# Gated linear attention's norm between its scores and states, keys loaded after the scores, and attention scores scaled in three turns

## The chip, the core and the metric

The kernel runs on one core of a Trainium2 chip. TensorE (PE) multiplies matrices, VectorE (DVE), ScalarE (ACT) and GpSimd (POOL) work on tiles, and SyncE (SP) issues nearly all transfers, one after the other in the order of its program. The metric is the device time of one launch in microseconds (us).

## The reference, cut to what matters

One decoder layer: a normed input is projected, differential softmax attention and gated linear attention (GLA) run side by side on the projections, each output is normed and gated, and one matrix projects both back.

```python
h = rms_norm(x, pre_g)
z = jnp.einsum('bsd,de->bse', h, w_in)
qa, ka, va, ga, qb, kb, vb, gb, gk_low = split_columns(z)
# differential attention, 8 heads, two maps each, in blocks of 128 queries
s = jnp.einsum('bqhmd,bkhmd->bhmqk', qb, k).astype(jnp.float32)
p = jax.nn.softmax(jnp.where(mask, s, -jnp.inf), axis=-1)
w = p[:, :, 0] - lam * p[:, :, 1]
out = jnp.einsum('bhqk,bkhv->bqhv', w.astype(v.dtype), v)
# gated linear attention, 4 heads, in chunks
attn = jnp.where(causal, jnp.einsum('bhnik,bhnjk->bhnij', q_dec, k_inv), 0.0)
o_intra = jnp.einsum('bhnij,bhnjv->bhniv', attn, v)
o = jnp.einsum('bhck,bhkv->bhcv', qd, state)
state = state * dl[..., None] + jnp.einsum('bhck,bhcv->bhkv', kt, vc)
ob = rms_norm(ob, gla_g).astype(x.dtype)
ob = ob.reshape(B, S, GLA_WIDTH) * jax.nn.silu(gb)
y = jnp.einsum('bse,ed->bsd', jnp.concatenate([oa, ob], axis=-1), w_out)
return x + rms_norm(y, post_g)
```

The sequence has 1024 rows, the model 1024 columns.

## The kernel before

Sums keep float32 quality by splitting each operand into a rounded part (hi) and a remainder (lo): every product is three matmul passes, hi*hi, lo*hi and hi*lo.

**Projections.** The input projection is a Strassen-like scheme: each pair of column blocks takes seven products of half-size blocks, named x, y and z after the PSUM bank that sums them. A product is twelve matmuls of 128x512. `order` lists the products; `go(n)` runs the next n of them, and after each it advances one background stream by one step. The weights of a product are loaded by SyncE (w_raw), rounded by ScalarE (line 327) and their remainder taken by VectorE (line 329). In the same time the output weights are split and stored back for later (wo_raw, wo_hi, wo_d), and finished projections are stored to DRAM (q_d and k_d for attention, g_d and gg_d for gates, gq_d and gv_d for GLA).

**GLA** is that background stream, the generator `gla()`. It runs over 4 heads with two halves of 512 rows each. Between two of its yields TensorE does one product, so a yield sets how much other work lies between two steps. The steps of a half are: transposed keys (matmuls pk), scores (pa, then masked on GpSimd), two steps of states (kv, added up in gu by VectorE), the norm of the half before (`gla_norm`), two steps of outputs (gpo, copied to the tile go by ScalarE, line 932), and the squares (sq), whose column sums end as a rounded part and remainder in the second half of tile gqd (called hl, line 943). The norm starts with the matmul gms over hl, then ScalarE takes the inverse root, VectorE scales and gates go, and four stores write it, split, to mixe (line 856). When `order` has eight products left, the stream is run to its end without products between.

The GLA tiles have one buffer each: go is in the buffer ks0, the gates gg in ks1, keys and queries kq in q0, decayed queries with hl (gqd) in q1, values gv in k0, masked scores with transposed keys (gan) in k1. The next half's go can be written only when the stores of the present go have read it.

**Attention** follows. It takes over the same buffers for the first head's q, k and ks (the lo/hi swapped keys), so these loads (`load_qk`, lines 964 and 967) wait for GLA's last uses, and SyncE waits with them. Three streams are merged by costs and due times (`merge`): `all_scores` (matmuls sc), `all_values` (transposes wtr, products po) and `out_early` (the output projection of GLA's part, ypart, from the weights wo_hi, wo_lo and the tiles m_hi, m_lo loaded from mixe). For a head's block of 128 queries, `scores` computes both maps; VectorE adds the mask and finds the minimum of the negated scores (line 1124), and ScalarE takes the exponent with its sum (line 1134). `scale_scores` then divides by the sums: a reciprocal, map two scaled on GpSimd by lambda (line 1153), and on VectorE map one scaled less map two (line 1154). A block is scaled in one call, behind the minima of the next block's first map, and its weights w are then free for the values.

TensorE's order is the code's order. On the other engines and SyncE a scheduler orders the instructions by its own simulated times, within their dependences and the places fixed by `issue_after`.

Of the kernel before, what the change touches and what calls it, by code (L numbers as in the profile page):

```python
# [14 lines left out]
P = 128  # L15
# [16 lines left out]
def hymba_kernel(  # L32
# [783 lines left out]
    decay(3)  # L816


    loaded = {}

    def gla_loads(g, half):

        if (g, half) not in loaded:
            qh = kp.tile([P, 2, 512], F32R, tag="q1", name="gqd")
            loaded[g, half] = [None, None, qh]
            if g < GLA_HEADS:
                cs = cols(half)
                kq = kp.tile([P, 2, 512], F32, tag="q0", name="kq")
                v = kp.tile([P, 4, 256], F32, tag="k0", name="gv")
                sp.dma_start(kq[:, 0], gq_d[g][2, :, cs])  # L830
                sp.dma_start(kq[:, 1], gq_d[g][0, :, cs])
                c0 = g % 2 * 256
                sp.dma_start(v, gv_d[g // 2][:, half * 4 : half * 4 + 4, c0 : c0 + 256])
                sp.dma_start(fp(qh[:, 0]), gq_d[g][1, :, cs])
                loaded[g, half][:2] = kq, v
        return loaded[g, half]

    def gla_norm(g, half, o, gates, hl):

# [21 lines left out]
    def gla():  # L861

        norm = None
        gla_loads(0, 0)
        yield
        yield
        for g, half in [(g, half) for g in range(GLA_HEADS) for half in range(2)]:
            cs = cols(half)
            kq, v, qh = gla_loads(g, half)
            qd = fp(qh[:, 0])  # L870
            if half == 0:
                u = None
# [9 lines left out]
            for i in range(4):  # L882
# [36 lines left out]
            for m in range(2):  # L919
# [12 lines left out]
                act.copy(o[:, :, m * 256 : m * 256 + 256], po)  # L932
                free.append(ib)
                yield
            hl = gla_loads(*((g, 1) if half == 0 else (g + 1, 0)))[2][:, 1]
# [159 lines left out]
    def scores(h, qb):  # L1095
# [6 lines left out]
        for m, p in enumerate((p0, p1)):  # L1102
            q = qk[h, "q", qb // 4][:, m, qc]
            parts = parts_of(n)
            if h == DA_HEADS - 1 and (qb, m) in ((1, 1), (0, 0), (0, 1)):

                parts = [(0, 512)]
            for i, (a, b) in enumerate(parts):
                sc = sc_bank("sc", [P, 512])
                for j, name in enumerate(("k", "ks")):  # L1110
                    for half in range(2):
                        lo, hi = max(a, half * 512), min(b, half * 512 + 512)
                        if lo < hi:
                            mm(
                                sc[:, lo - a : hi - a], q,
                                qk[h, name, half][:, m, lo - half * 512 : hi - half * 512],
                                start=(j == 0), stop=(j == 1),
                            )
                e = min(b, n)
                last = i == len(parts) - 1  # L1120

                behind = tc.issue_after(lowest[0]) if (h, qb) == (0, NT - 2) else nullcontext()
                with behind:
                    ins = dve.tensor_tensor_reduce(  # L1124
                        p[:, a:e], sc[:, : e - a],
                        maskt[:, NZ + P - (e - a) :] if last else maskt[:, : e - a],
                        1.0, 3e38 if i == 0 else st[:, 4 + m : 5 + m], ALU.add, ALU.min,
                        st[:, m : m + 1] if last else st[:, 4 + m : 5 + m],
                    )
# [12 lines left out]
                yield c  # L1142

    lowest, unscaled = [], []

    def scale_scores(after):

        if not unscaled:
            return 0.0
        h, qb, n, st, p0, p1 = unscaled.pop()  # L1150
        with tc.issue_after(after.ins) if after else nullcontext():
            dve.reciprocal(st[:, 4:6], st[:, 2:4])  # L1152
            pool.tensor_scalar(p1[:, :n], p1[:, :n], st[:, 5:6], lam, ALU.mult, ALU.mult)  # L1153
            dve.scalar_tensor_tensor(  # L1154
                p0[:, :n], p0[:, :n], st[:, 4:5], p1[:, :n], ALU.mult, ALU.subtract
            )
        w[h, qb] = p0
        return 0.25 + n / 1024 * 1.4

    def all_scores():  # L1160
        for h in range(DA_HEADS):
# [433 lines left out]
```

## Time and profile before

| | us |
|---|---|
| runs: median (lowest to highest, 3 runs) | 1017.77 (1012.45 to 1019.2) |
| the profiled execution, its own time | 1016.52 |
| its span, first to last instruction | 1014.8 |
| VectorE's product of scaled scores (line 1154), 64 of them: busy, and idle before | 53.0, 40.7 |
| ScalarE's copies to go (line 932), 16 of them: busy, and idle before | 8.7, 26.7 |
| TensorE's idle time before gms, two waits | 4.7 |

The profile is of one execution. A row of a stage gives the stretch in us, the sum, and then for TensorE, its weight loads (PEld), VectorE, ScalarE and GpSimd the busy time and in brackets the number of instructions, then the granted TensorE clock (1.00 is full), the share of the transfer engines' time, and GB/s. A row of the timeline gives start, duration, engine, line, operation, output<-inputs and, in square brackets, how long the engine had idled and what released it. SPq rows are SyncE issuing transfers. A row of the waits gives who waited, for whom, and total us, times and longest. In a row of transfers stand count, size and the median us from issue to landing.

### The profile page before, as it was taken

Reading aid. Unit: us, or ns where it says so; the run is one execution under the profiler, and the core shown is the slowest. Engines: PE = TensorE matmul, PEld = TensorE weight load, DVE = VectorE, ACT = ScalarE, POOL = GpSimd, SP = SyncE. Lnnn points to the kernel's source line nnn. Section 1 sums busy time; section 2 is a strip of 40 time slices with the busy share of each in tenths; the row PEclk is TensorE's granted clock in tenths of the full one; section 3 lists DMA queues with packets and bytes.
Section 4 is the critical chain, followed back from the end, with each engine's and each line's share of the span. In section 5 each row is a group of like instructions: output and inputs, shape, how many; then the busy total and the mean of one; then the engine's idle time right before and its main releaser. Section 6 shows DMA issues by size and latency. Waiting matters only on the chain.

```text
span 1014.8 us, 14875 instructions
## 1 busy us (share of the span) xinstructions
PE 967.4 (95%) x4866; PEld 809.3 (80%) x4866; DVE 737.2 (73%) x1450; ACT 589.1 (58%) x1152; POOL 142.0 (14%) x153
## 2 busy tenths in 40 slices
PE   6999999999999999999899889799999999999987
PEld 4878888778888888887788768578888888888765
DVE  5996477888898767867767775477777777777545
ACT  8642232446475476656567764257666667676664
POOL 5410000000000000000000000022222222343242
PEclk9999999999999999999999999899999999999999
DMA  9544333846757776689976779996566589875577
GB/s 334 200 114 150 119 110 110 237 115 161 265 182 242 256 228 220 211 248 289 288 232 213 249 250 317 324 337 204 187 223 214 165 310 352 262 192 96 129 214 139
DMA packets 156845, 220.38 MB, mean 217 GB/s; under 512 B 16240, under 2 KB 83824, under 8 KB 156672
## 3 DMA queue, kind: packets, MB, share of 16 engines
q1 hardware_dynamic: 152736, 212.10, 64.6%
q0 software_dynamic: 4032, 7.34, 4.8%
q8 instruction: 38, 0.62, 0.2%
q14 instruction: 39, 0.32, 0.1%
HBM read 133.93 MB, written 88.60 MB: 219 GB/s over the span
## 4 chain that ended last, share of the span: by engine, by line
PE 67%; DMA 17%; DVE 8%; ACT 4%; issue 3%; SPq 1%; POOL 0%; DVEq 0%; ACTq 0%; POOLq 0%
PE v L117 12%; PE ypart L117 11%; PE x L117 10%; PE z L117 7%; PE y L117 6%; PE sc L117 6%; PE po L117 5%; PE yps L117 4%; PE wtr L120 3%; DMA mixe<-go 2%; DMA v<-v_d 2%; DMA wo_d<-wo_raw 2%; DMA wo_raw<-in_w_out_dram 2%; DMA m_lo<-mixe 2%; DMA ks<-k_d 1%
## 5 line engine op out<-in xcount | busy, mean ns | idle before, releaser
L1134 ACT ACTIVATE p<-p,stt 128x896 f32<-128x896 f32 (+7 forms) x128 | 99.4, 777 | 60.0 <-DVE stt L1124 48.5
L329 DVE TENSOR_TENSOR w<-w_raw,w 128x512 fp32r<-128x512 f32 x134 | 91.4, 686 | 27.2 <-ACT w L327 26.7
L327 ACT CAST w<-w_raw 128x512 fp32r<-128x512 f32 x134 | 82.6, 619 | 39.4 <-PE y L117 19.0
L1153 POOL TENSOR_SCALAR p<-p,stt,lam 128x1024 f32<-128x1024 f32 (+3 forms) x64 | 56.3, 881 | 249.0 <-DVE stt L1152 244.2
L1124 DVE CUSTOM_DVE_ANT_0 p<-sc,maskt 128x512 f32<-128x512 f32 (+3 forms) x128 | 74.5, 586 | 20.5 <-PE sc L117 20.0
L117 PE MATMUL ypart<-wo_hi,m_hi 128*128 128x512 f32 x192 | 80.0, 417 | 5.5 <-issue 5.5
L117 PE MATMUL y<-h_hi,w 128*128 128x512 f32 x320 | 82.0, 399 | 0.6 <-ACT go L932 0.6
L1154 DVE SCALAR_TENSOR_TENSOR p<-p,stt,p 128x1024 f32<-128x1024 f32 (+3 forms) x64 | 53.0, 829 | 40.7 <-POOL p L1153 40.3
L117 PE MATMUL x<-s_hi,w 128*128 128x512 f32 x320 | 80.8, 395 | 1.7 <-ACT s L473 1.6
L117 PE MATMUL z<-s_hi,w 128*128 128x512 f32 x320 | 80.8, 395 | 1.4 <-DVE c L484 1.4
L117 PE MATMUL v<-w,s_hi 128*128 128x512 f32 x256 | 79.3, 390 | 0.6 <-DVE w L285 0.5
L117 PE MATMUL ypart<-wo_hi,m_lo 128*128 128x512 f32 x192 | 76.3, 398 | 0.5 <-DMA m_lo<-mixe 0.5
L117 PE MATMUL ypart<-wo_lo,m_hi 128*128 128x512 f32 x192 | 76.2, 397 | 0.0
L117 PE MATMUL sc<-k,q 128*128 128x512 f32 (+1 forms) x192 | 71.3, 374 | 1.4 <-DVE stt L1124 1.4
L117 PEld LDWEIGHTS x<-s_hi,w 128*128 128x128 f32 x320 | 58.9, 188 | 14.4 <-ACT s L473 2.7
L117 PEld LDWEIGHTS y<-h_hi,w 128*128 128x128 f32 x320 | 60.1, 191 | 12.9 <-ACT go L932 0.8
L117 PEld LDWEIGHTS z<-s_hi,w 128*128 128x128 f32 x320 | 58.9, 188 | 14.0 <-DVE c L484 2.5
L117 PE MATMUL sc<-ks,q 128*128 128x512 f32 (+1 forms) x192 | 66.8, 351 | 2.1 <-DMA ks<-k_d 2.1
L284 ACT CAST w<-w_block 128x1024 fp32r<-128x1024 f32 x24 | 25.2, 1052 | 66.9 <-PE v L117 42.0
L256 DVE TENSOR_TENSOR w_raw<-w_raw 128x512 f32<-128x512 f32 x80 | 55.9, 699 | 11.2 <-DMA w_raw<-in_w_in_dram 10.2
L117 PE MATMUL v<-w,h_hi 128*128 128x512 f32 x192 | 60.3, 401 | 0.7 <-ACT h_hi L567 0.7
L887 POOL TENSOR_SCALAR_AFFINE_SELECT gan<-gan 128x512 f32<-128x512 f32 x8 | 7.1, 888 | 383.7 <-ACT gan L886 383.7
(221 smaller groups left out, 2370.1 us busy)
## 6 DMA issues: line engine op xcount, KB each, us to landing
w_raw<-in_w_in_dram SPq DMA_DIRECT2D x40, 512.0 KB, 4.7
w_block<-in_w_in_dram SPq DMA_DIRECT2D x16, 512.0 KB, 4.1
k_d<-qk_st SPq DMA_DIRECT2D x64, 128.0 KB, 2.4
q_d<-qk_st SPq DMA_DIRECT2D x64, 128.0 KB, 2.7
wo_raw<-in_w_out_dram SPq DMA_DIRECT2D x32, 256.0 KB, 3.1
wo_d<-wo_hi SPq DMA_DIRECT2D x32, 256.0 KB, 2.5
wo_d<-wo_raw SPq DMA_DIRECT2D x32, 256.0 KB, 3.3
q<-q_d SPq DMA_DIRECT2D x32, 256.0 KB, 5.5
```

The costliest lines, as they stand in the source:

```text
L117: tc.keep_in_program_order(pe.matmul(*a, **k))
L120: tc.keep_in_program_order(pe.transpose(dst, src, ident))
L256: dve.tensor_tensor(dst, a, b, ALU.subtract)
L284: act.copy(w[0], src)
L327: act.copy(w[0], src)
L329: split_last[:] = [dve.tensor_tensor(w[1], src, fp(w[0]), ALU.subtract)]
L887: pool.affine_select(a, a, [[0, 4], [1, P]], ALU.is_ge, 0.0, base=0, channel_multiplier=-1)
L1124: ins = dve.tensor_tensor_reduce(p[:, a:e], sc[:, : e - a], maskt[:, NZ + P - (e - a) :] if last else maskt[:, : e - a], 1.0, 3e38 if i == ...
L1134: act.activation(p[:, :n], p[:, :n], AF.Exp, bias=st[:, m : m + 1], scale=-1.0, accum_out=st[:, 2 + m : 3 + m],)
L1153: pool.tensor_scalar(p1[:, :n], p1[:, :n], st[:, 5:6], lam, ALU.mult, ALU.mult)
L1154: dve.scalar_tensor_tensor(p0[:, :n], p0[:, :n], st[:, 4:5], p1[:, :n], ALU.mult, ALU.subtract)
```

## The change

Three edits.

1. In `gla()` the norm of the half before moves from behind the two steps of states to ahead of them, right behind the scores. The place where it stood becomes a bare yield, which every half now has, so each half takes one step more (the first half, which has no norm, too).
2. The keys and queries kq are loaded by a function of their own, `gla_keys`, called for the next half right after a half's scores, where they were loaded with values and decayed queries after the outputs.
3. `scale_scores` keeps a list. A block's reciprocal and GpSimd scaling are issued behind the next block's first map as before, VectorE's product behind the next block's second map, and the weights are released to the values one turn later. The cost that `merge` counts for it now stands with the block's own second map.

```diff
+    def gla_keys(n):
+        g, half = n // 2, n % 2
+        if g < GLA_HEADS and n not in keys:
+            kq = keys[n] = kp.tile([P, 2, 512], F32, tag="q0", name="kq")
+            for i, t in enumerate((2, 0)):
+                sp.dma_start(kq[:, i], gq_d[g][t, :, cols(half)])
...
             pool.affine_select(
                 a, a, [[0, 4], [1, P]], ALU.is_ge, 0.0, base=0, channel_multiplier=-1
             )
+            gla_keys(2 * g + half + 1)
             yield
+            if norm:
+                gla_norm(*norm)
+                yield
             us = [u]
             for m in range(2):
...
                 free.append(ib)
                 yield
-            if norm:
-                gla_norm(*norm)
-                yield
+            yield
             gates = kp.tile([P, 2, 512], F32, tag="ks1", name="gg")
...
                 if last:
-                    c += scale_scores(ins)
+                    scale_scores(ins)
                     if m:
-                        unscaled.append((h, qb, n, st, p0, p1))
+                        scaling.append([0, h, qb, n, st, p0, p1])
+                        c += 0.25 + n / 1024 * 1.4
                 yield c
...
+        done = [x for x in scaling if x[0] == 2]
+        for x in done:
+            scaling.remove(x)
+            w[x[1], x[2]] = x[5]
+        for x in scaling:
+            _, h, qb, n, st, p0, p1 = x
+            with tc.issue_after(after.ins) if after else nullcontext():
+                if x[0] == 0:
+                    dve.reciprocal(st[:, 4:6], st[:, 2:4])
+                    pool.tensor_scalar(
+                        p1[:, :n], p1[:, :n], st[:, 5:6], lam, ALU.mult, ALU.mult
+                    )
+                else:
+                    dve.scalar_tensor_tensor(
+                        p0[:, :n], p0[:, :n], st[:, 4:5], p1[:, :n], ALU.mult, ALU.subtract
+                    )
+            x[0] += 1
...
-        scale_scores(None)
+        for _ in range(3):
+            scale_scores(None)
```

**In the order: TensorE in a half of GLA.** The first rows are before, in the second half of the first head, from the first states to the first output matmul (a product is a row x8 with a row x4 behind it).

```order
L117 MATMUL kv<-gv,gan 128x128 x4
L117 MATMUL y<-h_hi,w 128x512 x8
L117 MATMUL y<-h_lo,w 128x512 x4
L117 MATMUL kv<-gv,gan 128x128 x2
L117 MATMUL z<-s_hi,w 128x512 x8
L117 MATMUL z<-s_lo,w 128x512 x4
L117 MATMUL gms<-gqd,ones 128x512
L117 MATMUL z<-s_hi,w 128x512 x8
L117 MATMUL z<-s_lo,w 128x512 x4
L117 MATMUL gpo<-gan,gv 128x128
```

The same half in the changed kernel, from the norm's matmul on; the next row is the first gpo.

```order
L117 MATMUL gms<-gqd,ones 128x512
L117 MATMUL z<-s_hi,w 128x512 x8
L117 MATMUL z<-s_lo,w 128x512 x4
L117 MATMUL kv<-gv,gan 128x128 x4
L117 MATMUL z<-s_hi,w 128x512 x8
L117 MATMUL z<-s_lo,w 128x512 x4
L117 MATMUL kv<-gv,gan 128x128 x2
L117 MATMUL x<-s_hi,w 128x512 x8
L117 MATMUL x<-s_lo,w 128x512 x4
L117 MATMUL y<-h_hi,w 128x512 x8
L117 MATMUL y<-h_lo,w 128x512 x4
```

Between gms and the first gpo stood one product, and now stand four products and both kv groups.

**TensorE and SyncE at GLA's end.** Before, the last gpo of all was followed by these rows up to the last gms; fourteen products came after it.

```order
L117 MATMUL gpo<-gqd,gu 128x128
L117 MATMUL x<-s_hi,w 128x512 x8
L117 MATMUL x<-s_lo,w 128x512 x4
L117 MATMUL y<-h_hi,w 128x512 x8
L117 MATMUL y<-h_lo,w 128x512 x4
L117 MATMUL x<-s_hi,w 128x512 x8
L117 MATMUL x<-s_lo,w 128x512 x4
L117 MATMUL x<-h_hi,w 128x512 x8
L117 MATMUL x<-h_lo,w 128x512 x4
L117 MATMUL gms<-gqd,ones 128x512
```

The same in the changed kernel; eight products come after it.

```order
L117 MATMUL gpo<-gqd,gu 128x128
L117 MATMUL y<-h_hi,w 128x512 x8
L117 MATMUL y<-h_lo,w 128x512 x4
L117 MATMUL z<-s_hi,w 128x512 x8
L117 MATMUL z<-s_lo,w 128x512 x4
L117 MATMUL gms<-gqd,ones 128x512
```

Four products stood between the last gpo and the last gms, and now two. SyncE before, from GLA's last two stores on; ten loads of wo follow (the last row is the first), then m_hi, m_lo and the eight stores of k_d.

```order
L856 DMA mixe<-go 128x4x128 x2
L967 DMA ks_5607<-k_d 64x512 x2
L393 DMA g_d<-g_st 128x512
L967 DMA ks_5607<-k_d 64x512 x2
L654 DMA wo_raw<-in_w_out_dram 128x512
L383 DMA q_d<-qk_st 64x512 x4
L967 DMA ks_5612<-k_d 64x512 x3
L650 DMA wo_d<-wo_hi 128x512
L967 DMA ks_5612<-k_d 64x512
L650 DMA wo_d<-wo_raw 128x512
L997 DMA wo_hi<-wo_d 128x1024
```

SyncE in the changed kernel at the same place (the first rows are the last of twelve loads of wo).

```order
L1004 DMA wo_hi<-wo_d 128x1024
L1004 DMA wo_lo<-wo_d 128x1024
L860 DMA mixe<-gg 128x4x128 x2
L860 DMA mixe<-go 128x4x128 x2
L1021 DMA m_hi<-mixe 128x1024
L1021 DMA m_lo<-mixe 128x1024
L383 DMA k_d<-qk_st 64x512 x8
L974 DMA ks_5607<-k_d 64x512 x4
L974 DMA ks_5612<-k_d 64x512 x4
```

The wo loads moved ahead of the last stores, the ks loads behind m and the k_d stores.

**VectorE at the start of attention.** Before, from the minima of the second block's first map on (p_5864 and p_5865 are the first block's maps; ISA rows with p are minima, those with stt alone read them out).

```order
L1124 ISA p_5891,stt<-sc,maskt,stt 128x384
L1124 ISA stt 128x1
L1152 RECIPROCAL stt<-stt 128x2
L1154 SCALAR_TENSOR_TENSOR p_5864<-p_5864,stt,p_5865 128x1024
L1124 ISA p_5892,stt<-sc,maskt 128x512
```

And in the changed kernel.

```order
L1131 ISA p_5897,stt<-sc,maskt,stt 128x384
L1131 ISA stt 128x1
L1164 RECIPROCAL stt<-stt 128x2
L1131 ISA p_5898,stt<-sc,maskt 128x512
L1131 ISA stt 128x1
L1131 ISA p_5898,stt<-sc,maskt,stt 128x384
L1131 ISA stt 128x1
L1169 SCALAR_TENSOR_TENSOR p_5864<-p_5864,stt,p_5865 128x1024
```

The second map's two minima now stand between the reciprocal and the product.

More of the change, by code (lines that the diff above doesn't have):

```diff
@@ L816, in hymba_kernel, with gla_loads @@
     decay(3)
[L819 to L825, printed above, removed]
+    keys, loaded = {}, {}
+    def gla_keys(n):
[4 more added lines that the diff above has]
+                sp.dma_start(kq[:, i], gq_d[g][t, :, cols(half)])
+    def gla_loads(n):
+        g, half = n // 2, n % 2
+        if n not in loaded:
+            v, qh = None, kp.tile([P, 2, 512], F32R, tag="q1", name="gqd")
             if g < GLA_HEADS:
-                cs = cols(half)
-                kq = kp.tile([P, 2, 512], F32, tag="q0", name="kq")
                 v = kp.tile([P, 4, 256], F32, tag="k0", name="gv")
-                sp.dma_start(kq[:, 0], gq_d[g][2, :, cs])
-                sp.dma_start(kq[:, 1], gq_d[g][0, :, cs])
                 c0 = g % 2 * 256
                 sp.dma_start(v, gv_d[g // 2][:, half * 4 : half * 4 + 4, c0 : c0 + 256])
-                sp.dma_start(fp(qh[:, 0]), gq_d[g][1, :, cs])
-                loaded[g, half][:2] = kq, v
-        return loaded[g, half]
+                sp.dma_start(fp(qh[:, 0]), gq_d[g][1, :, cols(half)])
+            loaded[n] = v, qh
+        return loaded[n]
     def gla_norm(g, half, o, gates, hl):
@@ L868, in gla @@
             cs = cols(half)
-            kq, v, qh = gla_loads(g, half)
+            (v, qh), kq = gla_loads(2 * g + half), keys[2 * g + half]
             qd = fp(qh[:, 0])
@@ L1138, in scores @@
                 if last:
-                    c += scale_scores(ins)
+                    scale_scores(ins)
                     if m:
-                        unscaled.append((h, qb, n, st, p0, p1))
+                        scaling.append([0, h, qb, n, st, p0, p1])
+                        c += 0.25 + n / 1024 * 1.4
                 yield c
-    lowest, unscaled = [], []
+    lowest, scaling = [], []
     def scale_scores(after):
[L1148 to L1158, printed above, removed]
+        done = [x for x in scaling if x[0] == 2]
[15 more added lines that the diff above has]
+            x[0] += 1
     def all_scores():
```

5 lines of the change are left out of this document (3 added, 2 removed).

## The prediction

> **What bounds the kernel now.** I read the page's busy shares first, then the busy time by stage, the list of what TensorE waited for, and then the timeline around each of those waits.
>
> ```profile
> PE 967.4 (95%) x4866; PEld 809.3 (80%) x4866; DVE 737.2 (73%) x1450; ACT 589.1 (58%) x1152; POOL 142.0 (14%) x153
> 500.00:550.00 50.00, 46.55 (x253) 39.63 (x252) 36.19 (x60) 33.15 (x62) 2.12 (x2) 1.00 0.73 241
> 550.00:600.00 50.00, 41.97 (x206) 34.64 (x206) 37.85 (x63) 36.49 (x68) 0.89 (x1) 0.98 0.76 246
> 600.00:650.00 50.00, 44.06 (x180) 35.50 (x180) 25.87 (x42) 18.21 (x31) 0.00 (x0) 0.92 0.92 313
> 690.00:850.00 160.00, 159.99 (x937) 139.15 (x936) 120.19 (x328) 108.75 (x241) 39.16 (x41) 1.00 0.67 225
> ```
>
> TensorE is the bound: 967.4 of 1014.8 us (the second column of a stage row is its busy time, the column before the last two the granted clock). The change adds and removes no matmul, so all that can be won is TensorE's idle time, 47 us in all, and clock lost after it. None of it lies in the middle of attention (159.99 of 160 us busy). 11.5 lie in the second half of GLA (500 to 600) and 5.9 where GLA ends and attention begins; the rest lies mostly before GLA and in the last 70 us, which the change doesn't touch. What ended the waits:
>
> ```profile
> PE gms L117 <- DVE gqd L943: 4.7, 2, 4.1
> PE kv L117 <- ACT go L932: 3.3, 1, 3.3
> PE kv L117 <- DMA gv<-gv_d: 2.7, 1, 2.7
>   DMA mixe<-go: 24.8, 6
> 540.77 0.40 PE L117 MATMUL gms<-gqd,ones 128*128 128x512 f32 x1
> 558.32 1.08 SPq L856 DMA_DIRECT2D mixe<-go  x1
> 564.71 1.07 ACT L932 COPY go<-gpo 128x512 f32<-128x512 f32 x2 [6.41 <-DMA mixe<-go]
> 565.35 1.16 PE L117 MATMUL kv<-gv,gan 128*128 128x128 f32 x8 [3.30 <-ACT go L932]
> 573.04 0.47 PE L117 MATMUL gms<-gqd,ones 128*128 128x512 f32 x1 [0.59 <-DVE gqd L943]
> 584.42 0.44 SPq L856 DMA_DIRECT2D mixe<-go  x1
> 589.51 1.08 ACT L932 COPY go<-gpo 128x512 f32<-128x512 f32 x2 [3.07 <-DMA mixe<-go]
> 596.85 0.69 DVE L943 TENSOR_TENSOR gqd<-sq,gqd 64x512 fp32r<-64x512 f32 x1
> 597.59 0.63 PE L117 MATMUL gms<-gqd,ones 128*128 128x512 f32 x1 [4.13 <-DVE gqd L943]
> 598.01 3.48 PE L117 MATMUL y<-h_hi,w 128*128 128x512 f32 x8
> 607.87 2.72 PE x L117 x12
> ```
>
> The fourth row is from the view of tile go: ScalarE's copies of the outputs into go stood still 24.8 us, six times, until the stores of the previous half's normed outputs had read the one go buffer. What ScalarE has queued behind such a copy (mask inputs, sums, weights) is late too. TensorE's idle from there: 3.3 before kv at 565.35; 2.7 before another kv, whose mask copy stood in ScalarE's queue behind such a go copy (the row blames gv's transfer); 0.59 at 573.04; 4.13 before the last gms; and 0.5 and 0.6 in two smaller cases. That is 11.8 us. After the 4.13 us the next eight matmuls took 3.48 instead of 2.07 us, 1.4 us of clock: 13.2 us together.
>
> **The change, part by part.** *The norm moves up.* Its number of instructions and transfers stays (per half one gms, two reads, four stores). From gms to the copy that its stores let go, 573.04 to 589.51, are 16.5 us. Today TensorE does one product between gms and the next gpo, 2.7 us by the last row above, and has the copy's input ready some 5 us after gms. Changed, four products (10.9), two kv groups and the gpo group lie between, about 14 us. So the wait shrinks from 11 us to some 2, which other work behind gpo covers; I leave 1.5 us in for halves whose stores are slow. gms itself now follows the last gpo by four products in all halves but the last, 10.9 us; the chain from go copy to gqd took 8.0 (589.51 to 597.54). That holds.
>
> *The last gms.* Each half has one step more, so the interleaving runs out later: after the last gpo there are now two products (5.4 us) before the last gms, where there were four. Without the wait in front, the chain of 8.0 us starts at once, half a microsecond shorter since only one copy is left: 7.5 - 5.4 = 2.1 us of stall. ScalarE's queue decides the rest: nothing if it is emptier than at 589.51, up to 7 if the cast of wo_hi that stands inside the chain waits for its load. I take 2.5. Whether the clock drops after it is open; after 1.87 us of idling it did:
>
> ```profile
> 948.85 0.51 PE L117 MATMUL yps<-wo_hi,m_hi 128*128 128x512 f32 x1 [1.87 <-ACT yps L1447]
> 951.58 0.63 PE L117 MATMUL yps<-wo_lo,m_hi 128*128 128x512 f32 x1
> 952.84 0.40 PE L117 MATMUL yps<-wo_lo,m_hi 128*128 128x512 f32 x1
> ```
>
> At 951.58 a matmul takes 0.63 us, at 952.84 0.40 again. I count 1.4 us, as after the 4.13. The Trainium skill, "TensorE: Matmul & The Clock Gate", section "What's actually happening", has the clock halve only after an idle window of about 3.4 us; by it this 1.4 would be 0 and the forecast 1001.6; the row at 948.85 speaks against it here, and the row decides. GLA so: 13.2 - 1.5 - 2.5 - 1.4 = 7.8 us gained, between 3 (stall of 7) and 13.2 (nothing left).
>
> *Keys.* The same two transfers per half, issued once pa has read the old ones rather than with the values. No wait of TensorE on kq is in the trace, so the gain is nothing; they leave the moment of gv, gqd and the stores, and SyncE runs in order: bounds 0.5 us to either side.
>
> *Where GLA ends.* The last norm now stands eight products before the first ypart instead of fourteen, and SyncE's order turns round: weights wo first, then the last stores of mixe, mixe's loads m at once, the eight k_d stores, and only then the eight ks loads.
>
> ```profile
> 611.06 1.36 SPq L856 DMA_DIRECT2D mixe<-go  x2
> 612.52 1.42 SPq L967 DMA_DIRECT2D ks<-k_d  x2
> 633.35 0.32 SPq L1014 DMA_DIRECT2D m_hi<-mixe  x1
> 628.95 1.35 DVE L379 SCALAR_TENSOR_TENSOR qk_st<-c,qk_st 128x512 fp32r<-128x512 f32 x2
> 635.80 9.11 SPq L383 DMA_DIRECT2D k_d<-qk_st  x8
> 643.27 0.77 PE L117 MATMUL ypart<-wo_hi,m_hi 128*128 128x512 f32 x1 [5.48 <-issue]
> 644.49 0.79 PE L117 MATMUL ypart<-wo_hi,m_lo 128*128 128x512 f32 x1 [0.46 <-DMA m_lo<-mixe]
> 645.00:650.00 5.00, 5.00 (x15) 3.87 (x14) 0.70 (x2) 0.00 (x0) 0.00 (x0) 0.60 0.87 258
> 650.00:655.00 5.00, 5.00 (x23) 3.92 (x22) 3.44 (x11) 3.20 (x5) 0.56 (x1) 1.00 0.96 353
> 630.85 0.32 SPq L997 DMA_DIRECT2D wo_hi<-wo_d  x1
> ks<-k_d SPq DMA_DIRECT2D x64, 128.0 KB, 6.0
> ```
>
> Today the products end at 637.8 (643.27 less the 5.48) and attention starts at 643.27: 5.9 us idle (5.48 that the profile calls issue, but in which m was still landing, and 0.46), then 15 matmuls in 5 us where 23 is the rate, 1.7 us, and 0.8 on the first two: 8.4 us. The loads of m left only at 633.35, behind ks loads that waited for go and gates to be stored and behind ten wo loads. Changed: stores about 9 to 12 us after the last gms (573.04 to 584.42 is 11.4), m issued behind them and landed by 18 to 20, products done at 22.2 (0.4 and eight times 2.72). So m should be there. The ks loads are late next: their stores' data come from the fourth product after gms, 11.3 us, and today are done 3.4 us after it (630.3, four products before 637.8), so 14.7. Eight stores at 0.5 us end at 18.7; of the ks loads the first score wants the fifth and sixth, out at 21 and in at 27 with the 6.0 us of the last row. TensorE, six ypart and one sc matmul after its products, asks at 23.8. 3.3 us idle, 3.5 with a little clock: gain 4.9 us. Bounds: 8.4 (ks in time) and a loss, for which see the rivals.
>
> *Scores scaled in three turns.* The same 64 reciprocals, 64 POOL scalings and 64 VectorE products; the product no longer stands right behind POOL's scaling but behind the second map's minima.
>
> ```profile
> DVE p L1154 <- POOL p L1153: 40.3, 41, 1.4
> 655.68 1.29 DVE L1154 SCALAR_TENSOR_TENSOR p<-p,stt,p 128x1024 f32<-128x1024 f32 x1 [1.35 <-POOL p L1153]
> 657.63 0.38 PE L117 MATMUL sc<-k,q 128*128 128x256 f32 x1 [1.39 <-DVE stt L1124]
> 663.97 0.63 PE L120 MATMUL wtr<-ident,p 128*128 128x128 f32 x4 [1.71 <-DVE p L1154]
> 680.57 0.47 PE L117 MATMUL sc<-ks,q 128*128 128x512 f32 x1 [0.59 <-DMA ks<-k_d]
> 610.00:690.00 80.00, 70.36 (x339) 57.83 (x338) 44.55 (x110) 33.97 (x70) 8.34 (x9) 0.96 0.96 325
> ```
>
> VectorE's 40.3 us of waiting for POOL go, and nearly all of it is worth nothing, since TensorE has no gap there. Only the two gaps at the start hang on it: 1.39 us before sc (minima behind the first wait for POOL), and 1.71 before wtr, where the product is behind one minimum more but without POOL in front. I take 1.5 off the two; at most 3.1 off, at worst 1 more for a later product. wtr keeps its places in TensorE's order, score products move back by about ten, so the values find their weights as before; if that cover failed, each of the 32 groups of values could cost up to the 1.3 us of a product, but wtr waits once in the whole trace, so I count nothing.
>
> The sum: 7.8 + 4.9 + 1.5 = 14.2 us off the profiled execution's 1016.5 gives 1002.3. That execution is 1.3 us below the median of 1017.77, so 1003 us against the median.
>
> **The rivals.** *The copies still wait.* From the gms at 540.77 to its last store at 558.32 went 17.5 us, more than the 14 now between; and DMA shares of 0.73 to 0.92 in these stages won't fall if the same bytes pass in less time. Then GLA gains its lower bound 3, the join 4.9: 1016.5 - 7.9, and 1.3 for the median, about 1010. For it: copies wait six times today. Against it: the room before gpo grows by three products in every half.
>
> *The transfers are the bound.* From 610 to 690 the DMA engines are 0.96 busy, and at 680.57 TensorE waits for the second head's ks. If that landing doesn't move, all gained before it is given back there: 1016 to 1018. Against it: in the new order the twelve wo loads stand before the last stores, not behind them, so part of these 26 MB (80 us at 325 GB/s) moves ahead, where shares of 0.73 and 0.76 leave room.
>
> *Slower: the last norm is too late.* Today last gms to first ypart takes 45.7 us (597.59 to 643.27). With eight products behind it only 22.2 us are covered. If that chain stayed 45.7, TensorE would idle 23.5 us, with 2.5 of clock 26, where 8.4 are lost now: 17.6 lost against 9.3 gained, 1026. It decides from a chain of 37 us on. For it: the k_d stores, behind which ks now stands, took 9.11 us for eight. Against it: between stores and m stood 20 us of other issues, which are gone from there, and that pace came from the backlog of wo loads at 630.85.
>
> **How the numbers follow.** The forecast, 1003, with its own bounds from 993 (13.2, 8.4 and 3.1 gained) to 1009 (3, 4.9 and 0.5): 0.62. Copies still wait, 1010: 0.18. Transfers bind, 1017: 0.12. Last norm too late, 1026: 0.08. About 1%, 10 us, can be told from no change here: faster means below 1007.6, slower above 1028. Of the forecast 0.55 lies below 1007.6, of the second case 0.07: faster 0.62. Slower is only the far part of the last case, 0.05, and the same 0.33. The range 994 to 1017 leaves out the last case, half of the third, and a little below.
>
> **What would show it.** Right: the waits of go copies on mixe below 8 us in place of 24.8; no idle over 2 us in GLA but for the last gms; first ypart within 2 us of the last product, ks the next wait; VectorE's wait for POOL near zero, with no change of TensorE's busy time between 690 and 850. Wrong: a last gms that stalls over 5 us; a first score that waits over 8 us for ks; the second head's ks landing as late as now.

## The result, and the profile after

The changed kernel took 1008.08 us (median of 8 runs, 1004.3 to 1015.33); the kernel before, in the same series, 1018.49 us (8 runs, 1012.45 to 1022.74). The ratio is 0.9899, 95% interval 0.9864 to 0.9934. In a second series it was 0.9951 (0.9924 to 0.9977): 1009.39 us (12 runs) against 1015.55 (33 runs). The changed kernel came to 1008 to 1009 both times; it is the kernel before that lay between 1014.5 and 1018.5 from series to series. So the change is worth 6 to 10 us, and the forecast's 1003 was 5 to 6 us too low. The profiled execution took 1006.61 us, its span 1004.9, against 1016.52 and 1014.8 before.

Busy time after, first over the span and then by stage (columns as before the change):

```profile
PE 964.7 (96%) x4866; PEld 809.7 (81%) x4866; DVE 737.9 (73%) x1450; ACT 589.9 (59%) x1152; POOL 144.0 (14%) x153
```

```profile
500.00:550.00 50.00, 48.83 (x253) 41.21 (x252) 38.39 (x61) 37.04 (x70) 1.61 (x2) 1.00 0.75 245
550.00:600.00 50.00, 49.66 (x266) 42.37 (x264) 40.68 (x68) 34.99 (x65) 0.63 (x1) 1.00 0.80 259
600.00:650.00 50.00, 40.06 (x161) 31.93 (x161) 26.33 (x55) 19.42 (x33) 2.28 (x2) 0.93 0.96 324
690.00:850.00 160.00, 158.68 (x927) 138.49 (x926) 118.44 (x328) 110.11 (x242) 44.89 (x45) 1.00 0.72 237
```

The second half of GLA, 500 to 600, idles 1.5 us where it idled 11.5. The next 50 us idle 9.9 where they idled 5.9. The border flatters the first pair: the wait before the last gms lies ahead of 600 in the kernel before (4.13 us, ended at 597.59) and behind it now. From 500 to 650 together it is 11.4 us in place of 17.4. What ended TensorE's waits, VectorE's and ScalarE's (who waited, for whom: us, times, longest):

```profile
PE gms L117 <- DVE gqd L950: 6.2, 2, 5.1
PE sc L117 <- DMA ks<-k_d: 6.1, 2, 4.0
PE wtr L120 <- DVE p L1169: 2.9, 2, 1.7
DVE p L1169 <- POOL p L1165: 12.2, 16, 2.4
  DMA mixe<-go: 11.6, 5
```

Two waits of TensorE are new in size, the one before the last gms and the one for ks; VectorE's wait for GpSimd fell from 40.3 to 12.2 us, and the go copies' wait from 24.8 to 11.6. TensorE's timeline at those places, and ScalarE's between the last go copy and the last gms:

```profile
604.74 0.79 PE L117 MATMUL gms<-gqd,ones 128*128 128x512 f32 x1 [5.07 <-DVE gqd L950]
605.33 3.33 PE L117 MATMUL x<-s_hi,w 128*128 128x512 f32 x8
609.41 2.00 PE L117 MATMUL x<-s_hi,w 128*128 128x512 f32 x8
...
628.48 0.39 PE L117 MATMUL ypart<-wo_hi,m_hi 128*128 128x512 f32 x1
634.66 0.47 PE L117 MATMUL sc<-ks,q 128*128 128x512 f32 x1 [4.04 <-DMA ks<-k_d]
635.79 0.63 PE L117 MATMUL ypart<-wo_hi,m_hi 128*128 128x512 f32 x1
```

```profile
594.79 0.60 ACT L939 COPY go<-gpo 128x512 f32<-128x512 f32 x1
596.98 0.62 ACT L327 CAST w<-w_raw 128x512 fp32r<-128x512 f32 x1 [1.59 <-PE y L117]
601.34 0.62 ACT L646 CAST wo_hi<-wo_raw 128x512 fp32r<-128x512 f32 x1 [2.16 <-DMA wo_raw<-in_w_out_dram]
601.98 0.62 ACT L947 COPY sq<-sq 64x512 f32<-64x512 f32 x1
603.35 0.62 ACT L949 CAST gqd<-sq 64x512 fp32r<-64x512 f32 x1
```

The last gms comes 9.95 us after its go copy began; inside that stand a cast of w, which waited 1.59 us for TensorE's product y, and a cast of wo_hi, which waited 2.16 us for a transfer; neither has anything to do with GLA. After the 5.07 us the next eight matmuls take 3.33 us instead of 2.00. The products end at 628.48, where they ended at 637.8, and m is there at once; ks is not. SyncE at that place:

```profile
618.58 3.72 SPq L1021 DMA_DIRECT2D m_hi<-mixe  x1
622.87 5.23 SPq L383 DMA_DIRECT2D k_d<-qk_st  x8
```

The ks loads follow at 628.15.

### The profile page after: what moved, and what is told of

Its sections match the earlier page's. It is cut to its first block, busy times and chain, and to the rows that moved or that the text cites. A ratio compares the mean times of both kernels' runs of the same rounds, so it can differ in the third digit from the quotient of the medians.

```text
span 1004.9 us, 14892 instructions
## 1 busy us (share of the span) xinstructions
PE 964.7 (96%) x4866; PEld 809.7 (81%) x4866; DVE 737.9 (73%) x1450; ACT 589.9 (59%) x1152; POOL 144.0 (14%) x153
## 4 chain that ended last, share of the span: by engine, by line
PE 73%; DMA 9%; DVE 8%; ACT 4%; issue 3%; SPq 1%; POOL 1%; DVEq 0%; ACTq 0%; POOLq 0%
PE x L117 13%; PE v L117 12%; PE ypart L117 11%; PE y L117 8%; PE z L117 8%; PE sc L117 6%; PE po L117 5%; PE yps L117 4%; PE wtr L120 2%; PE gpo L117 2%; DMA w_raw<-in_w_in_dram 2%; DMA k<-k_d 1%; PE kv L117 1%; DMA v_d<-v_hi 1%; DMA wo_d<-wo_raw 1%
## 5 line engine op out<-in xcount | busy, mean ns | idle before, releaser
L1165 POOL TENSOR_SCALAR p<-p,stt,lam 128x1024 f32<-128x1024 f32 (+3 forms) x64 | 61.4, 960 | 204.7 <-DVE stt L1164 190.4
L117 PEld LDWEIGHTS y<-h_hi,w 128*128 128x128 f32 x320 | 59.0, 188 | 11.6
L256 DVE TENSOR_TENSOR w_raw<-w_raw 128x512 f32<-128x512 f32 x80 | 55.7, 698 | 11.8 <-DMA w_raw<-in_w_in_dram 10.7
L473 ACT COPY s<-x 128x512 f32<-128x512 f32 x60 | 34.9, 581 | 48.4 <-PE x L117 44.0
L1169 DVE SCALAR_TENSOR_TENSOR p<-p,stt,p 128x1024 f32<-128x1024 f32 (+3 forms) x64 | 53.5, 836 | 12.5 <-POOL p L1165 12.2
```

Of the source, the lines that this page charges most:

```text
L117: tc.keep_in_program_order(pe.matmul(*a, **k))
L256: dve.tensor_tensor(dst, a, b, ALU.subtract)
L473: act.copy(b[k], ps)
L1169: dve.scalar_tensor_tensor(p0[:, :n], p0[:, :n], st[:, 4:5], p1[:, :n], ALU.mult, ALU.subtract)
```

## The experiments

The table has three series on three chips, each with the kernel before on the same chip. "Products end" is the moment in the profiled execution when the last product before attention is done (the first ypart's start less its idle time), and "then" what remains of the span.

| kernel | median us | before | ratio (95%) | products end | then |
|---|---|---|---|---|---|
| norm alone | 1010.82 | 1014.53 | 0.997 (0.995 to 0.999) | 632.6 | 371.4 |
| keys alone | 1021.04 | 1014.53 | 1.0074 (1.0048 to 1.01) | 639.3 | 385.0 |
| scores' turns alone | 1014.07 | 1014.53 | 1.000 (0.9978 to 1.0021) | 636.9 | 375.1 |
| norm and keys | 1011.06 | 1014.53 | 0.9973 (0.9951 to 0.9995) | 633.5 | 376.7 |
| the whole change again | 1009.39 | 1015.55 | 0.9951 (0.9924 to 0.9977) | 633.8 | 374.9 |
| norm and scores' turns | 1011.95 | 1015.55 | 0.9961 (0.9935 to 0.9986) | 633.3 | 371.2 |
| whole, ks ahead of k_d | 1009.09 | 1015.55 | 0.9941 (0.9914 to 0.9968) | 635.4 | 374.7 |
| whole, no empty step | 1007.91 | 1015.55 | 0.9927 (0.9902 to 0.9953) | 623.6 | 381.0 |
| that, ks behind m | 1006.35 | 1016.60 | 0.9905 (0.9876 to 0.9934) | 625.1 | 378.3 |
| that, last wo behind ks too | 1006.94 | 1016.60 | 0.9904 (0.9879 to 0.9929) | 627.1 | 380.9 |
| norm alone, no empty step | 1008.71 | 1016.60 | 0.9922 (0.9898 to 0.9945) | 626.1 | 380.6 |

The first execution of the whole change ended its products at 628.5 and needed 376.4 us then; the kernel before 637.8 and 377.0. One profiled execution is uncertain by some us: the same GLA code ended its products at 628.5 and at 633.8, 5.3 us apart. And the profiled executions of the norm alone and of norm and scores' turns were the fastest of their series, 5 to 6 us under the median, those of the keys alone and of the last wo behind ks the slowest, 5 and 3 us over it.

**The parts by themselves.** The norm with its extra step, the keys and the scores' turns were each put into the kernel before; a fourth kernel is the whole change without the scores' turns. The edit of the first:

```diff
@@ before: gla()
+            if norm:
+                gla_norm(*norm)
+                yield
             us = [u]
...
-            if norm:
-                gla_norm(*norm)
-                yield
+            yield
```

> Only the norm's move (with the step it adds to each half); keys and scores as before. Theory A (norm carries all, the scores' turns cost a little): 9 to 12 us below the kernel before, so at or 1 to 2 us under the whole change; the waits of go copies on mixe near 11.6 us as in the whole change. Theory B (the forecast's split: scores worth 1.5 us, norm the rest): 8 to 9 us below before, 1 to 2 us over the whole change. Theory C (the keys must come sooner or the moved norm can't pay): under 5 us below before, with a wait of TensorE's on kq in GLA that neither kernel has.

> Only the keys' transfers are issued sooner. Theories A and B: within 1 us of before, go copies still waiting about 25 us on mixe. Theory C gives no gain here either, but then the move of the norm alone must fall short. A loss of 2 us or more would say that the sooner keys delay gv or the stores.

> Only the scaling of the scores in three turns. Theory B: 1.5 us below before, from the gaps of 1.39 and 1.71 us at the start of attention. Theory A: 0 to 2 us above before, since the second turn's product stands later than the weights' transposes want it (waits of wtr on p summing to over 2.5 us instead of 1.71). Both: VectorE's 40.3 us of waiting for POOL falls to some 12, and TensorE's busy time from 690 to 850 stays within 1 us of 160.

> The norm's move and the sooner keys, scores scaled as before. Theory A: 10 to 12 us below before, 0 to 2 us under the whole change. Theory B: 8 to 9 us below before, 1 to 2 us over the whole change. If it equals the norm's move alone within 1 us, the keys are worth nothing here.

The norm alone gives 1 to 5 us, less than theory A or B expected. Theory C named that size, but its mark, a wait on kq, isn't in the trace, and adding the keys (0.9973) changes nothing. The keys alone cost 5 to 10 us. In GLA the trace shows one cause, a wait for values that left later (before, the longest such wait was 2.7 us). SyncE, and then TensorE:

```profile
463.25 5.70 SPq L383 DMA_DIRECT2D k_d<-qk_st  x8
470.17 0.40 SPq L837 DMA_DIRECT2D gv<-gv_d  x1
475.10 2.04 PE L117 MATMUL kv<-gv,gan 128*128 128x128 f32 x8 [5.99 <-DMA gv<-gv_d]
```

The values stood behind eight stores of k_d; in the kernel before, the same half's had left at 460.88, ahead of those stores. So the sooner keys changed the order of SyncE's queue, and they are not themselves what the values waited for. That and the other waits put the products' end 1.5 us later; the other 8 us of this execution, 5 us over its median, lie in attention, and why the sooner keys would bring those stayed open.

The scores' turns alone are worth nothing, between 2.2 us less and 2.1 more. TensorE's waits there:

```profile
PE wtr L120 <- DVE p L1162: 2.9, 2, 1.7
PE po L117 <- DVE wt_lo L1201: 1.7, 4, 0.6
PE wtr L120 <- DVE wt_lo L1201: 0.9, 1, 0.9
PE sc L117 <- DVE stt L1124: 0.5, 1, 0.5
```

The gap before sc shrank from 1.39 to 0.49 us, as was hoped. But wtr keeps its 1.71 and waits a second time, 1.2 us, and the transposes' copies (wt_lo), behind the later products on VectorE, are waited for by 2.6 us. Some 0.9 us won against 3.8 of new small waits; the runs can't tell the remainder from nothing.

**The whole change again, and without the keys.** Parts of 0.997, 1.007 and 1.000 don't make 0.9899, so the whole change was run again, and the norm with the scores' turns:

> The whole change once more, unaltered, in one series with the other three here, since norm and keys without the scores' turns came to a ratio of 0.9973 on one chip while the whole change had 0.9899 in its own series, and the scores' turns alone had 1.000. Theory A (three parts that add up: norm 3 to 4 us, keys nothing, scores nothing, and the rest of the 10 us was the series): 0.995 to 0.999, that is 2 to 5 us below before. Theory D (the parts help each other: the scores' turns are worth 7 us only once the norm has moved): 0.988 to 0.992, that is 8 to 12 us below.

> The norm's move and the scores in three turns, keys loaded where they were. Theory A: the norm's move alone, 2 to 5 us below before. Theory D: as the whole change, 8 to 12 us below, if the keys are worth nothing; 2 to 5 below only if the keys are what the scores' turns need, for which no mechanism is known.

The whole change came to 0.9951 and the pair to 0.9961, as theory A had it. There is no interplay of 7 us; most of the difference was the level of the kernel before in the first series. The repeat's GLA (TensorE's timeline, with its ks wait):

```profile
516.91 0.47 PE L117 MATMUL gms<-gqd,ones 128*128 128x512 f32 x1 [2.67 <-DVE gqd L950]
609.04 0.80 PE L117 MATMUL gms<-gqd,ones 128*128 128x512 f32 x1 [5.46 <-DVE gqd L950]
633.82 0.39 PE L117 MATMUL ypart<-wo_hi,m_hi 128*128 128x512 f32 x1
638.75 0.76 PE L117 MATMUL sc<-ks,q 128*128 128x512 f32 x1 [2.79 <-DMA ks<-k_d]
```

and the two go copies that these gms hang on (ScalarE):

```profile
505.11 0.59 ACT L939 COPY go<-gpo 128x512 f32<-128x512 f32 x1
598.88 0.60 ACT L939 COPY go<-gpo 128x512 f32<-128x512 f32 x1
```

From copy to gms are 11.8 and 10.2 us, not 8.0.

**The ks loads ahead of the stores they don't need.** The whole change, with the first head's ks loads issued behind m and their place fixed:

```diff
@@ whole change: before attention
-    for n in ("q", "k", "ks"):
+    for n in ("q", "k"):
...
     mix0 = mix(0)
+    for half in (1, 0):
+        load_qk(0, "ks", half)
     go(3)
```

> The whole change, with the first head's eight ks loads issued right behind the loads of m and ahead of the eight k_d stores, which they don't need. If the ks wait of 4.04 us in the join comes from standing behind those stores (5.23 us on the queue): the wait falls under 1.5 us, its slow matmuls go with it, and the time falls 3 to 6 us against the whole change. If the ks loads are held by the last mixe stores or by the DMA engines being full: the wait stays within 1 us and the time within 1.5 us.

The ks wait is gone, and with it the slow matmuls. The time hardly moved (1009.09 against 1009.39): what was won is waited out 21 us later, for the first values.

```profile
637.37 0.39 PE L117 MATMUL sc<-ks,q 128*128 128x512 f32 x1
...
658.88 0.55 PE L117 MATMUL po<-wt_hi,v 128*128 128x256 f32 x1 [3.56 <-DMA v<-v_d]
```

So the cause of the ks wait was the k_d stores, as expected, but removing it was worth nothing, which neither side had foreseen.

**Without the empty step.** The bare yield where the norm stood is left out, so four products stand again between the last go copy and the last gms, and fourteen behind it.

```diff
@@ whole change: gla()
                 free.append(ib)
                 yield
-            yield
             gates = kp.tile([P, 2, 512], F32, tag="ks1", name="gg")
```

> The whole change without the empty step that each half got, so that again four products stand between the last go copy and the last gms, and fourteen behind it. Theory A for the end of GLA: the stall at the last gms and the ks wait are one thing, a chain from the last go copy to ks with too few products beside it; with four more beside it the 5.07 us and its 1.3 us of clock go, the ks wait falls under 1 us, and the time falls 6 to 11 us against the whole change, unless the go copies wait longer on mixe again (over 16 us in all). Rival: what is won at gms comes back at the first ypart, which waits 3 to 6 us for m as in the kernel before: 2 to 5 us below the whole change.

> Only the norm's move, without the empty step, keys and scores as before: the smallest edit that might hold the whole gain. If the empty step costs what the last gms loses and the keys give nothing: as the whole change without that step, 0.991 to 0.994. If the keys' earlier loads are what lets half after half start in time once the empty step is gone: 0.996 to 1.000, with waits of kv on gv or of pk on kq in GLA over 2 us in all.

The stall at the last gms vanishes, and the products end 10 us sooner than in the repeat, at 623.6. Not only do four products cover the chain from go copy to gqd again, it is also shorter, 6.0 us (575.60 to 581.59). Then TensorE stands before m, whose loads left at 619.84 behind four ks loads and five of wo, and the rival came about, if with a smaller gain:

```profile
628.02 0.47 PE L117 MATMUL ypart<-wo_hi,m_hi 128*128 128x512 f32 x1 [4.47 <-DMA m_hi<-mixe]
```

For m_lo it waits another 1.24 us. In time this kernel can't be told from the whole change (1007.91 and 1009.39, the intervals overlap). The norm alone without the empty step has 0.9922 (to 0.9945) against 0.997 (from 0.995) with it. These intervals miss each other by 0.0005, and they come from two series on two chips, while the whole change differed by 0.005 between two series; so that the empty step costs time is likely and not shown. In that smallest edit the go copies wait on mixe as much as before the change, and TensorE's GLA still runs 11.7 us faster:

```profile
  DMA mixe<-go: 24.8, 7
```

**m, ks and wo in the order in which they are wanted.** To the kernel without the empty step came the ks edit above; in a second kernel also the last four wo loads of twelve went behind ks.

```diff
@@ second kernel
-    for e in range(E, E + 6):
+    for e in range(E, E + 4):
         weights(e)
...
+    weights(E + 4)
+    weights(E + 5)
     go(3)
```

> The whole change without the empty step, and the eight ks loads issued behind the loads of m. Without the ks loads in front of them the loads of m leave 3 us earlier than in the run without the empty step (there m_hi left at 619.84 and landed at 628.02). Theory E (the join is set by SyncE's order alone): the first ypart's waits of 4.47 and 1.24 us shrink to under 3 together, with under 1 us on ks, and the time falls 2 to 5 us below the kernel without the empty step, to a ratio of 0.987 to 0.991. Theory F (behind the join the queue of SyncE and the memory tiles of v are the bound, so that time won at the join is waited out before the first values): the join's waits shrink as said, but po then waits 3 to 6 us for v and the ratio stays at 0.991 to 0.994.

> As the run with m before ks, and the last four of the twelve wo loads (2 MB) behind ks too, so that m leaves right after its stores. Theory E: no wait over 1 us at the first ypart, 0 to 3 us for ks, ratio 0.983 to 0.988. Theory F: no wait at the first ypart either, but waits for v of 4 to 8 us, and a ratio of 0.990 to 0.994, the same as without the empty step.

Theory F came about, if with slightly lower ratios. The waits at the join fall from 5.7 us to 1.9 and 0.8 in the first kernel and to 1.4 for ks in the second, and the first values wait longer instead. The first kernel, TensorE, and then SyncE:

```profile
627.43 0.50 PE L117 MATMUL ypart<-wo_hi,m_lo 128*128 128x512 f32 x1 [1.93 <-DMA m_lo<-mixe]
627.77 0.40 PE L117 MATMUL ypart<-wo_lo,m_hi 128*128 128x512 f32 x1
629.88 0.47 PE L117 MATMUL sc<-ks,q 128*128 128x512 f32 x1 [0.80 <-DMA ks<-k_d]
653.07 0.55 PE L117 MATMUL po<-wt_hi,v 128*128 128x256 f32 x1 [5.15 <-DMA v<-v_d]
```

```profile
628.88 5.23 SPq L383 DMA_DIRECT2D k_d<-qk_st  x8
...
636.27 7.31 SPq L383 DMA_DIRECT2D q_d<-qk_st  x8
643.68 2.48 SPq L383 DMA_DIRECT2D k_d<-qk_st  x4
646.25 2.48 SPq L383 DMA_DIRECT2D q_d<-qk_st  x4
648.78 1.07 SPq L1084 DMA_DIRECT2D v<-v_d  x2
```

In the second kernel the same po waits 6.79 us. In all four kernels without the empty step v leaves between 648.8 and 649.8, whether the products ended at 623.6 or at 627.1. In the first execution of the whole change, products done at 628.48, it left at 648.97 as well, and there no po waited for it. Behind k_d SyncE issues without a pause for 20 us, and the transfer engines are full meanwhile (the first kernel by stretches, the share before the last column):

```profile
630.00:643.00 13.00, 12.51 (x57) 10.05 (x57) 9.01 (x28) 6.28 (x11) 2.29 (x2) 1.00 0.91 283
643.00:649.00 6.00, 3.21 (x19) 2.59 (x18) 4.22 (x12) 2.81 (x7) 0.99 (x1) 1.00 0.93 269
649.00:653.00 4.00, 0.00 (x0) 0.00 (x0) 1.02 (x2) 0.51 (x2) 0.00 (x0) 0.73 0.96 297
```

**Fewer, larger stores.** Is it the number of issues or the bytes that hold v back? In the first of those kernels the last q and k stores were written as one transfer for both halves of the partitions:

```diff
@@ m and ks first: take()
-                for m in range(2):
-                    ins = sp.dma_start(d[m, t, :, cs], fp(src)[64 * m : 64 * m + 64])
+                if ending:
+                    tc.keep_in_program_order(sp.dma_start(d[:, t, :, cs], fp(src)))
```

> The run with m and ks first, with the queue's last stores of q and k, 24 of 128 KB each behind m, written as 12 of 256 KB (both halves of the partitions in one). In that run v left at 648.78, behind 20 us in which the queue issued k_d, wo, q_d, k_d and q_d stores without a pause, and po waited 5.15 us for it. Theory F1 (the queue issues too many transfers, 0.65 us each): v leaves 5 to 9 us earlier, po's wait falls under 1.5 us, and the ratio falls by 0.003 to 0.006, to 0.985 to 0.988. Theory F2 (the same bytes take their time on the DMA engines, or v waits for the stores to land): each merged store takes twice as long on the queue or v stays put, po still waits 4 us or more, ratio 0.989 to 0.992.

Neither theory: 1053.42 us, ratio 1.0366 (1.0328 to 1.0404). TensorE stood 40.9 us before the first values, and a merged store took five times as long on the queue as a half, not twice.

```profile
647.19 17.92 SPq L383 DMA_DIRECT2D q_d<-qk_st  x4
665.21 8.47 SPq L383 DMA_DIRECT2D k_d<-qk_st  x2
673.77 12.15 SPq L383 DMA_DIRECT2D q_d<-qk_st  x2
```

```profile
665.00:686.00 21.00, 0.00 (x0) 0.00 (x0) 0.00 (x0) 0.00 (x0) 0.00 (x0) 0.50 0.13 51
```

From 665 to 686 SyncE issues nothing but these stores, and 0.13 of the sixteen engines' time is busy, as much as two engines have. The target of such a store is a block of 2 by 64 by 512. The Trainium skill, "DMA: Bandwidth & Descriptors", section "Rules for kernel authors", says that an outermost dimension smaller than 16 confines a transfer to at most as many engines as it has entries, here 2 of 16, or 0.125; the row agrees. The kernel thus measures another thing than it was meant to, and whether issues or bytes hold v back stays open; the full engines of 630 to 653 speak for the bytes.

## Why the prediction was right, and where it was off

The direction and the range held (994 to 1017); the size did not. Of the 14.2 us that were added up, 6 to 10 came, which is at the bound of 1% in the one series and under it in the other. (The sum gives 1003.6; it was rounded down to 1003.) That the first series came nearest is in part luck: the kernel before was 3 us slower there than in the second.

The miss shows when the sum is split by place. Up to the products' end 7.8 us were forecast, and behind it 6.4, 4.9 for the join and 1.5 for the scores. In the first execution 9.3 and 0.6 came (377.0 behind it became 376.4), in the repeat 4.0 and 2.1. In both the part behind the products' end fell short, and in the repeat GLA's part too.

**The norm moves up: the gain is there, one price was too low.** In the five other executions with the norm moved and the empty step the products' end moved by 2.4 to 5.2 us, in the first by 9.3. The step that failed in GLA is "the chain from go copy to gqd took 8.0 (589.51 to 597.54). That holds": one instance, from a place where no cast that isn't part of the chain made it wait in ScalarE's queue. It measured 9.95 and 10.2 us at the last gms, 11.8 in a middle half of the repeat, and 6.0 without the empty step. So the last gms stalled 5.07 and 5.46 us and not 2.5 (within the 7 that was named for a cast of wo_hi that waits, which is part of what the first trace shows). A stall over 5 us was a named sign of being wrong, and it came in all six executions (5.07 to 5.74). A middle half, which was to be covered, stalled another 2.67: its last copy began 3.2 us after the last gpo, since the other copy of the pair had waited 2.09 us for mixe, and the chain took 11.8, against 12.3 us of TensorE's work beside both. The clock term was right: 3.33 us less 2.00 is 1.3, against 1.4.

One reading of the kernel before was wrong: the 2.7 us before kv were put down to a mask copy behind a go copy. In the code kv reads the transposed keys and the values, not the masked scores. The keys' copy had ended at 500.92; gv had left at 498.05, and its loads take 5.7 us in the median. So the row that blames gv was right, and these 2.7 us were not the go copies'.

**The empty step was costed as a stall, and was worth more at the products' end.** Without it the products end 10.7 to 14.2 us sooner than before, near the whole 13.2 that was called removable. The prediction did see that the step takes two products from the front of the last gms; the traces show that this, with the longer chain, is what separates the kernels with it from 13.2. In the time of the whole kernel no such difference is shown.

**The marker was wrong.** The forecast wanted the go copies' waits below 8 us. They were 11.6, and in the kernel with the norm alone and no empty step 24.8 as before, with the products done 11.7 us sooner. So "the wait shrinks from 11 us to some 2" is not the step on which the gain hangs. The reading that fits, though no run tests it, is that the move buys not a copy that waits less, but more matmuls that TensorE has to do between gms and the work behind the copy. For the same reason the rival "the copies still wait", whose 1010 is nearer to the 1008 to 1009 measured than 1003, has the number by luck: where the copies waited as long as before, GLA was not slower for it.

**The join** was forecast at 3.5 us left of 8.4. Left were 4.04 us and about 1.5 of clock in the first execution (the matmuls of 0.63 us from 635.79 to 638.78 come every 0.43 us instead of every 0.23), so that 2.9 us were gained and not 4.9, and 2.79 in the repeat, with slow matmuls behind it too. The step that failed is "Eight stores at 0.5 us end at 18.7": they ended 23.4 us after the last gms, since they left at 622.87, behind m's loads, the first of which held the queue for 3.72 us, and took 0.65 each. The order of causes was as told, m there, ks late behind the k_d stores, which the kernel with ks in front of them shows.

**The scores' three turns** were forecast at 1.5 us off and are worth nothing that can be measured. "wtr waits once in the whole trace, so I count nothing" failed: the cover of the values was thin just there, and the later product is waited for at wtr and, through VectorE's queue, at wt_lo. Between 690 and 850, where TensorE had idled nothing, it now idles 1.3 us.

**The keys** cost nothing with the norm moved, as forecast; alone they cost 5 to 10 us.

**The rival "the transfers are the bound"** had 0.12, and part of it came. It was looked for at the second head's ks. There it bit in the first execution, 2.07 us where it had been 0.59, with a clock of 0.94 from 660 to 690 in place of 1.00:

```profile
668.86 0.47 PE L117 MATMUL sc<-k,q 128*128 128x512 f32 x1 [2.07 <-DMA ks<-k_d]
```

With the eight slow matmuls behind it, up to 673.02, that costs some 3 us by estimate, about what the join had won. Yet this ks came 11.7 us sooner than before, so it did not land "as late as now", and in the repeat it held up nothing there. In the kernels without the empty step the transfers bite sooner: at m (5.7 us in the whole change without it), and, where m comes in time, at the first values (5.15 and 6.79). The column "then" of the table agrees: kernels whose products end at 623 to 627 need 378 to 381 us then, the ones that end at 632 to 635 need 371 to 377. These differences are not much larger than what one execution is uncertain by.

**The clock.** The slow matmuls after the last gms came after an idle time of 5.07 us. In the kernel with norm and scores' turns they came after 2.63 (granted clock 0.84 from 635 to 640):

```profile
635.09 0.40 PE L117 MATMUL sc<-k,q 128*128 128x512 f32 x1
638.11 0.48 PE L117 MATMUL sc<-ks,q 128*128 128x512 f32 x1 [2.63 <-DMA ks<-k_d]
638.82 0.63 PE L117 MATMUL ypart<-wo_hi,m_lo 128*128 128x512 f32 x1
```

After the 1.93 us at 627.43 above, the next ypart took 0.40, and in the kernel before, after the 3.30 us at 565.35, the next eight matmuls of 128x512 took 2.09 us together, the full rate. So the length of the one idle time does not decide it here. The Trainium skill, "TensorE: Matmul & The Clock Gate", section "What's actually happening", has the clock halve only after an idle window of about 3.4 us; the 2.63 us here don't bear that out, as the 1.87 in the prediction did not.

No version is shown to beat the whole change: the best two, 1006.35 and 1006.94 us, have ratios of 0.9905 and 0.9904, whose intervals overlap both of its own.

## What to carry to other kernels

Before a gain upstream is counted, look for the first point downstream whose time is set by something else (here ks, m or the first values, behind a full queue of transfers), and count only up to it. Price a chain through a shared engine from several of its instances, not from one, since what the scheduler puts between its links belongs to its length. And when a step of an interleaving is moved, look at the number of steps: an empty one changes what stands beside the last, uncovered chain (here 10 us at the products' end, of which nothing that can be told was left in the time of the whole kernel).

## What the runs showed that was not expected

Two stores of 64 by 512 written as one of 2 by 64 by 512 made the queue take 4.5 us for each (17.92 for four) where each half had taken 0.9 (7.31 for eight), at 51 GB/s from 665 to 686 against some 270 to 280 in the kernel with the halves, and the kernel came out 38 us over the kernel before. And the kernel before, unaltered, had medians of 1018.49, 1014.53, 1015.55, 1016.60 and 1015.03 us in five series, the last four on four chips: a ratio of 0.99 from one series of 8 runs was 0.995 in the next.
